# An encoder layer with latent attention in one kernel: x tiles, weight buffers, DMA issuers, output weights and the last norm rearranged

## The chip, the cores and the metric

The kernel runs on one core of a Trainium2 chip. The metric is the device time of one execution in microseconds; a run of the kernel before gives the median of several executions. Beside the times there is a profile of one execution, taken by the hardware profiler.

The engines of a core work side by side, each through its own list of instructions in order: TensorE (PE) for matmuls, VectorE (DVE), ScalarE (ACT), GpSimd (POOL), and SyncE (SP), which here only issues DMAs. ACT can issue DMAs too. PEld in the profile is the load of a matmul's stationary operand. A line L59 is line 59 of the kernel before.

## The reference, cut to what matters

DEPTH is 1, so only the attention layer and the final norm are computed. Input x has 1024 rows of 1024 columns in float32.

```python
h = x + mla_mixer(rms_norm(x, l0_norm), *weights)
return rms_norm(h, final_norm)

def mla_mixer(h, w_in, q_norm, w_uq, kv_norm, w_ukv, w_out):
    proj = h @ w_in                       # c_q 384, c_kv 256, k_pe 64, gate 1024
    q = rms_norm(c_q, q_norm) @ w_uq      # 8 heads of 128 + 64 (rotary)
    kv = rms_norm(c_kv, kv_norm) @ w_ukv  # 8 heads of 128 (key) + 128 (value)
    s = q_nope @ k_nope.T + rope(q_pe) @ rope(k_pe).T
    o = softmax(s * scale) @ v            # not causal
    return (o * silu(gate)) @ w_out
```

rms_norm(y, g) is y * rsqrt(mean(y * y) + 1e-6) * g.

## The kernel before

Every product is made of three matmuls (`mm3`, L58): each float32 operand is split into a high part that the PE's format holds and a low part for the rest, and high x high, high x low and low x high are summed. `split` (L63) does it for a weight: POOL writes the high part, DVE subtracts it for the low one. So each weight goes DMA, POOL, DVE, PE, and has a raw buffer and a pair of split buffers.

The instructions are written down in one order, but a planner puts those of each engine into the order in which they stand in its queue, by a simulated timeline and the written order as priority; a load can go out far ahead of its place in the program once its buffer is free. Buffers are named tiles of pools with a number of copies (`bufs`). Writing a copy again waits until its readers are done.

The stages:

1. **Latent query** (L161 to L186). Eight steps over the 1024 columns of x. Each loads a 128 x 1024 tile of x transposed (`xr`) and 128 x 384 of weights, scales and splits both (ACT writes `xh`, DVE `xl`), and does 18 matmuls into six accumulators. The first tile is loaded and split in two halves, the others whole.
2. **Streams** (`stream`, L251). The other columns of w_in, 128 at a time: two for the latent key and value, one for the rotary key, eight for the gate. Each uses two half weights (`gwh`, `gwl`, in four copies each, pool `gp`), 24 matmuls a half. The latent norms and the rotary queries (`rope_half`, L343, two groups of four heads in two halves of the rows) lie between the gate streams. `load_q(wqp[...])` at L375 loads the rotary weights, two for a group; they share the tags `wq_h`, `wq_l` (two copies) and the raw buffer `w_r` (one copy) with the query and key weights of the heads. `rope_half` stores its results, high and low, to `qpe_d` in DRAM by four DMAs on SP's queue (L362).
3. **Attention** (L634 to L699). 64 units, eight heads of eight row blocks, numbered u. `scores(u)` does 10 matmuls into one of two score buffers, DVE takes the maximum, ACT the exponential (L464), POOL scales, DVE transposes 32 x 32 blocks. After four units `exchange` (L473) finishes the transposition of a group by 16 DMAs on SP's queue, eight for each half `d`. `split_part` (L483) splits `d` on ACT, DVE and POOL, and `values` (L498) multiplies with v. Keys, queries and values of the next head are produced in between. In the second unit of the last head, `load_w_out` (L517) loads and splits all eight half blocks of w_out for the first 512 output columns, on ACT and on DVE or POOL.
4. **Output** (L538 to L630, L700). For each row block and half of the columns: split of the gated heads (`o_split`), 24 matmuls, plus x, sum of squares. The blocks 0 to 3 of the first half start in the last units of attention. The last row block (`out_last`, L606) does its second half in two chunks; behind its last matmul come the sum of squares, the reciprocal root with one Newton step (`rsqrt`, L138), and the scaling and storing of both halves:

```python
v = ss/D + v ; s = sqrt(v) ; r = 1/s             # DVE, ACT, DVE
s = -0.5*r*r ; s = s*v ; r = (s + 1.5)*r         # DVE
```

Of the kernel before, what the change touches and what calls it, by code (L numbers as in the profile page):

```python
# [8 lines left out]
F32 = mybir.dt.float32  # L9
F32R = mybir.dt.float32r  # L10
AF = mybir.ActivationFunctionType
ALU = mybir.AluOpType
AX = mybir.AxisListType

P = 128
# [14 lines left out]
def kernel(  # L30
# [56 lines left out]


    g_sb = const.tile([P, KD + 5], F32, name="g_sb")
    const.tile([P, 72], F32, name="pad_a")  # L90
    qpe_d = dram.tile([H, 4, 32, L], F32, name="qpe_d")

    row_d = {name: dram.tile([P, KD], F32, name=f"{name}_d") for name in ("rx", "sq", "sk", "rq", "rk")}
    kk_h = const.tile([P, L], F32R, name="kk_h")
    kk_l = const.tile([P, L], F32R, name="kk_l")
    ss = const.tile([P, 2, KD], F32, name="ss")
    const.tile([P, 112], F32, name="pad_b")

    def acc(name):
        return ps_a.tile([P, 512], F32, name=name, tag="acc")  # L100
# [15 lines left out]

    xctx = ExitStack()
    xs = xctx.enter_context(tc.tile_pool(name="xs", bufs=1, side="right"))
    gp = xctx.enter_context(tc.tile_pool(name="gp", bufs=4, side="right"))
    xp = xctx.enter_context(tc.tile_pool(name="xp", bufs=1, side="right"))  # L120
    xh = xp.tile([P, KD, L], F32R, name="xh")
    xl = xp.tile([P, KD, L], F32R, name="xl")
# [23 lines left out]
    with ExitStack() as wctx:  # L146
        wp = wctx.enter_context(tc.tile_pool(name="wp", bufs=3))

        idle = wp.tile([P, HT], mybir.dt.bfloat16, name="idle", bufs=1)
        nc.vector.memset(idle, 0.0)  # L150
        warm = ps_t.tile([P, HT], F32, name="warm", tag="t")
        for _ in range(8):
            mm(warm, lhsT=idle[:, 0:P], rhs=idle, start=True, stop=True)
        ones_f = wp.tile([P, P], F32, name="ones_f", bufs=1)
        nc.vector.memset(ones_f, 1.0)
        ones = xs.tile([P, P], F32R, name="ones")
        nc.scalar.copy(ones, ones_f)
        s_a, s_b = wide("s_a"), wide("s_b")
        a_4, a_5 = acc("acc_4"), acc("acc_5")
        accs = [[s_a[:, 0:512], s_a[:, 512:L]], [s_b[:, 0:512], s_b[:, 512:L]], [a_4, a_5]]  # L160
        for k in range(KD):  # L161
            wr = wp.tile([P, QR], F32, name=f"wr_{k}", tag="wr")
            xr = wp.tile([P, L], F32, name=f"xr_{k}", tag="xr")
            if k == 0:
                nc.scalar.dma_start(g_sb, gains)
                nc.sync.dma_start(xr[:, halves(0)], xT[0:P, halves(0)])
                nc.sync.dma_start(wr, wcq[k])
                nc.sync.dma_start(xr[:, halves(1)], xT[0:P, halves(1)])
            else:
                nc.sync.dma_start(wr, wcq[k])  # L170
                nc.sync.dma_start(xr, xT[k * P:(k + 1) * P])
            wh = wp.tile([P, QR], F32R, name=f"wh_{k}", tag="wh")
            wl = wp.tile([P, QR], F32R, name=f"wl_{k}", tag="wl")
            split(wr, wh, wl)
            for hs in [halves(0), halves(1)] if k == 0 else [slice(0, L)]:
                nc.scalar.activation(xh[:, k, hs], xr[:, hs], AF.Copy, scale=g_sb[:, k:k + 1])
                nc.vector.scalar_tensor_tensor(
                    xl[:, k, hs], xr[:, hs], g_sb[:, k:k + 1], f32(xh[:, k, hs]),
                    op0=ALU.mult, op1=ALU.subtract,
                )  # L180
            units = [(m, half) for half in range(2) for m in range(3)]
            if k == KD - 1:
                units = [(m, half) for m in range(3) for half in range(2)]
            for m, half in units:
                ms, hs = slice(m * P, (m + 1) * P), halves(half)
                mm3(accs[m][half], wh[:, ms], wl[:, ms], xh[:, k, hs], xl[:, k, hs], k == 0, k == KD - 1)  # L186

        nc.scalar.copy(craw[0], s_a)
        nc.vector.tensor_copy(craw[1], s_b)
        nc.scalar.copy(craw[2][:, 0:HT], a_4)  # L190
        nc.vector.tensor_copy(craw[2][:, HT:L], a_5)
# [129 lines left out]
    def load_split(shape, src, tag, bufs, pool=None):  # L321
        pool = pool or wts
        wh = pool.tile(shape, F32R, name=f"{tag}_h", tag=f"{tag}_h", bufs=bufs)
        wl = pool.tile(shape, F32R, name=f"{tag}_l", tag=f"{tag}_l", bufs=bufs)
        wr = wts.tile(shape, F32, name=f"{tag}_r", tag="w_r")
        nc.sync.dma_start(wr, src)
        split(wr, wh, wl)
        return wh, wl

    def load_q(src):  # L330
        return load_split([P, 3, P], src, "wq", 2)

    def load_k(h):
        return load_split([P, 2, P], wuk[h], "wk", 1)
# [8 lines left out]
    def rope_half(g, half, w):  # L343
# [8 lines left out]
        for i, (f0, f1, op) in enumerate(((cos, sin, ALU.subtract), (sin, cos, ALU.add))):  # L352
            t, hl = rooms[((g * 2 + half) * 2 + i) % len(rooms)]
            t0, t1 = t[:, 0:HT], t[:, HT:L]
            hi, lo = hl[:, 0:HT], hl[:, HT:L]
            nc.vector.tensor_mul(t0, ab[0], f0)
            nc.vector.tensor_mul(t1, ab[1], f1)
            nc.gpsimd.tensor_tensor(t0, t0, t1, op=op)
            nc.scalar.copy(hi.bitcast(F32R), t0)
            nc.vector.tensor_sub(lo.bitcast(F32R), t0, hi)  # L360
            for c, src in ((i, hi), (2 + i, lo)):
                nc.sync.dma_start(qpe_d[g * 4:(g + 1) * 4, c, :, hs], src)  # L362

    for i in range(1, H):
        stream_gate(i)
# [79 lines left out]
    produce_v(v_now, 0, w_v)  # L445

    square, part = {}, {}

    def scores(u, q, kx, qpe):
        half, qs = (u % 8) // 4, slice((u % 4) * P, (u % 4 + 1) * P)  # L450
# [22 lines left out]
    def exchange(g):  # L473

        src = square.pop(g).rearrange("p j k t c -> p j (k t c)")
        for two in range(2):
            d = part[g, two] = at.tile([P, 2, L], F32, name="d", tag="d")
            for a in range(2):
                for j in range(4):
                    r0 = (two * 2 + a) * 32  # L480
                    nc.sync.dma_start(d[j * 32:(j + 1) * 32, a], src[r0:r0 + 32, j])

    def split_part(g, two):  # L483
        d = part[g, two]
# [113 lines left out]
            nc.vector.scalar_tensor_tensor(v, ss[:, 1, t:t + 1], 1.0 / D, v, op0=ALU.mult, op1=ALU.add)  # L598

    def out_rstd(t):  # L600
        mean_square(t, 1)
        s, r = (columns.tile([P, 1], F32, name=f"y{c}", tag=f"y{c}", bufs=2) for c in "sr")
        rsqrt(ss[:, 0, t:t + 1], s, r)
        return r

    def out_last(t):  # L606
# [17 lines left out]
                mean_square(t, 1)  # L624
        r = out_rstd(t)
        y0 = y_sb[:, t * HT:(t + 1) * HT]
        nc.scalar.mul(y0, y0, r)
        nc.scalar.dma_start(out[ts, halves(0)], y0)
        nc.vector.tensor_scalar(yg, yg, r, 1.0, op0=ALU.mult, op1=ALU.mult)
        nc.sync.dma_start(out[ts, halves(1)], yg)  # L630
    v_of = {0: v_now}
    U = H * 8
    w_q_next, w_k_next = load_q(wqn[1]), load_k(1)
    for u in range(U + 10):  # L634
        h, i = u // 8, u % 8
# [18 lines left out]
        if u % 2 == 0 and u >= 8:  # L654
            g, two = (u - 8) // 4, (u - 8) % 4 // 2
            if g < U // 4:
                values(g, two, v_of[g // 4])
        if u == U + 1:
            y_sb = turned_tile("y_sb").rearrange("p a b -> p (a b)")
            gf_sb = wop.tile([P, D], F32, name="gf_sb")  # L660
            nc.sync.dma_start(gf_sb, gf)
        if u in (U + 1, U + 3):
            started.append(out_start(0, len(started)))
        if u == U + 3:
# [15 lines left out]
            if i in (4, 5, 6):  # L680
                produce_v(v_now, i - 3, w_v)
        if h == H - 1:
            if i == 1:
                for k in range(H):
                    load_w_out(k, 0)
            continue
        if i == 3:
            produce_k(k_next, 0, w_k_next)
# [76 lines left out]
```

## Time and profile before

| | us |
|---|---|
| median of 3 runs | 598.67 (598.4 to 599.02) |
| the profiled execution | 599.3 |
| its span, first to last instruction | 597.3 |
| PE busy in the span | 579.0 |
| DVE, ACT, POOL busy | 433.0, 277.3, 218.9 |
| mean granted clock of PE | 0.992 |

In the timeline a row has the start, the duration, the engine and line, the operation and its tiles, out<-in, with their shape; in brackets stands how long the engine had been idle and what ended that. "x16" says that 16 like instructions are merged into the row. SPq and ACTq are the DMA issues of SP and ACT. A matmul's start is exact, its end is modelled, so matmuls in a row overlap; the time of one is the distance between starts. The list of waits has the engine and line that waited, for whom, the sum in us, how many times, and the longest.

### The profile page before, as it was taken

Reading aid. Unit: us, or ns where it says so; the run is one execution under the profiler, and the core shown is the slowest. Engines: PE = TensorE matmul, PEld = TensorE weight load, DVE = VectorE, ACT = ScalarE, POOL = GpSimd, SP = SyncE. Lnnn points to the kernel's source line nnn. Section 1 sums busy time; section 2 is a strip of 40 time slices with the busy share of each in tenths; the row PEclk is TensorE's granted clock in tenths of the full one; section 3 lists DMA queues with packets and bytes.
Section 4 is the critical chain, followed back from the end, with each engine's and each line's share of the span. In section 5 each row is a group of like instructions: output and inputs, shape, how many; then the busy total and the mean of one; then the engine's idle time right before and its main releaser. Section 6 shows DMA issues by size and latency. Waiting matters only on the chain.

```text
span 597.3 us, 8664 instructions
## 1 busy us (share of the span) xinstructions
PE 579.0 (97%) x2988; PEld 494.0 (83%) x2988; DVE 433.0 (72%) x632; ACT 277.3 (46%) x435; POOL 218.9 (37%) x195
## 2 busy tenths in 40 slices
PE   8999999979999998999999999999999989999995
PEld 5888888858888887888988989888888968978885
DVE  5813579926205889899878899898987996783663
ACT  4347553111103464456454545454545673653642
POOL 3414504514101344544334354434442662563000
PEclk9999999979999999999999999999999999999999
DMA  8846322233202166466654747456646975431332
GB/s 300 277 128 233 106 75 68 64 143 109 108 18 71 40 160 146 110 148 153 145 128 107 180 107 160 93 115 166 143 93 138 275 174 141 120 104 53 124 140 105
DMA packets 35534, 78.71 MB, mean 132 GB/s; under 512 B 7266, under 2 KB 10850, under 8 KB 35428
## 3 DMA queue, kind: packets, MB, share of 16 engines
q1 hardware_dynamic: 34196, 76.08, 47.3%
q10 hardware_dynamic: 1296, 2.10, 1.0%
q8 instruction: 23, 0.38, 0.3%
q14 instruction: 19, 0.16, 0.1%
HBM read 36.19 MB, written 8.41 MB: 75 GB/s over the span
## 4 chain that ended last, share of the span: by engine, by line
PE 77%; DVE 8%; DMA 6%; issue 3%; SPq 2%; ACT 2%; POOL 0%; ACTq 0%; DVEq 0%; POOLq 0%
PE s L59 4%; PE s L60 4%; PE s L456 4%; PE pv L59 4%; PE s L457 4%; PE s L61 4%; PE pv L60 4%; PE pv L61 4%; PE o L61 4%; PE o L60 4%; PE g L59 4%; PE g L60 4%; PE o L59 4%; PE g L61 4%; PE q L60 2%
## 5 line engine op out<-in xcount | busy, mean ns | idle before, releaser
L470 POOL TENSOR_SCALAR probs<-probs,rc 128x1024 f32<-128x1024 f32 x64 | 80.9, 1268 | 111.0 <-DVE rc L469 85.3
L464 ACT ACTIVATE probs<-s,nmx 128x1024 f32<-128x1024 f32 x64 | 71.3, 1114 | 72.8 <-DVE nmx L462 69.5
L489 ACT CAST pt_h<-d 128x1024 fp32r<-128x1024 f32 x64 | 66.0, 1051 | 46.3 <-PE pv L61 19.9
L471 DVE STREAM_TRANSPOSE probs<-probs 128x1024 f32<-128x1024 f32 x64 | 78.9, 1233 | 6.5 <-POOL probs L470 5.9
L462 DVE TENSOR_REDUCE nmx<-s 128x1 f32<-128x1024 f32 x64 | 76.9, 1207 | 7.5 <-PE s L457 7.4
L59 PE MATMUL pv<-pt_h,v_h 128*128 128x256 f32 x256 | 72.6, 284 | 2.3 <-ACT pt_h L489 2.3
L60 PE MATMUL pv<-pt_l,v_h 128*128 128x256 f32 x256 | 72.5, 283 | 0.6 <-DVE pt_l L491 0.5
L61 PE MATMUL pv<-pt_h,v_l 128*128 128x256 f32 x256 | 72.4, 283 | 0.0
L494 POOL TENSOR_TENSOR pt_l<-d,pt_h 128x512 fp32r<-128x512 f32 x32 | 46.0, 1438 | 46.1 <-ACT pt_h L489 29.4
L59 PE MATMUL g<-xh,gwh 128*128 128x512 f32 x160 | 62.8, 392 | 0.0
L60 PE MATMUL g<-xl,gwh 128*128 128x512 f32 x160 | 62.7, 392 | 0.0
L61 PE MATMUL g<-xh,gwl 128*128 128x512 f32 x160 | 62.5, 391 | 0.0
L59 PEld LDWEIGHTS pv<-pt_h,v_h 128*128 128x128 f32 x256 | 48.9, 191 | 4.4 <-ACT pt_h L489 3.2
L59 PE MATMUL s<-k_h,q_h 128*128 128x512 f32 x128 | 50.1, 394 | 1.9 <-ACT probs L464 1.9
L60 PEld LDWEIGHTS pv<-pt_l,v_h 128*128 128x128 f32 x256 | 48.9, 191 | 2.9 <-DVE pt_l L491 0.8
L61 PEld LDWEIGHTS pv<-pt_h,v_l 128*128 128x128 f32 x256 | 48.9, 191 | 2.0
L60 PE MATMUL s<-k_l,q_h 128*128 128x512 f32 x128 | 50.3, 393 | 0.0
L456 PE MATMUL s<-kk_h,qpe 128*128 128x512 f32 x128 | 50.2, 392 | 0.0
L457 PE MATMUL s<-kk_l,qpe 128*128 128x512 f32 x128 | 50.1, 391 | 0.0
L61 PE MATMUL s<-k_h,q_l 128*128 128x512 f32 x128 | 49.9, 390 | 0.0
L491 DVE TENSOR_TENSOR pt_l<-d,pt_h 128x1024 fp32r<-128x1024 f32 x32 | 45.1, 1410 | 5.2 <-ACT pt_h L489 4.6
L60 PE MATMUL o<-wol,o_split 128*128 128x512 f32 (+1 forms) x118 | 44.8, 379 | 0.0
(191 smaller groups left out, 1293.0 us busy)
## 6 DMA issues: line engine op xcount, KB each, us to landing
d<-probs SPq DMA_DIRECT2D x256, 128.0 KB
gwr<-in_wg SPq DMA_DIRECT2D x20, 256.0 KB
craw_b<-in_x SPq DMA_DIRECT2D x8, 512.0 KB
qpe<-qpe_d SPq DMA_DIRECT2D x16, 256.0 KB
wor<-in_wo SPq DMA_DIRECT2D x16, 256.0 KB
xr<-in_x SPq DMA_DIRECT2D x16, 256.0 KB
xr<-in_xT SPq DMA_DIRECT2D x7, 512.0 KB
qpe_d<-craw_a SPq DMA_DIRECT2D x8, 256.0 KB
```

The costliest lines, as they stand in the source:

```text
L59: mm(ps, lhsT=lh, rhs=rh, start=first, stop=False)
L60: mm(ps, lhsT=lh, rhs=rl, start=False, stop=False)
L61: mm(ps, lhsT=ll, rhs=rh, start=False, stop=last)
L456: mm(s[:, ks], lhsT=qpe_s, rhs=kk_h[:, ks], start=False, stop=False)
L457: mm(s[:, ks], lhsT=qpe_s, rhs=kk_l[:, ks], start=False, stop=True)
L462: nc.vector.tensor_reduce(nmx, s, axis=AX.X, op=ALU.max, negate=True)
L464: nc.scalar.activation(p_t.rearrange("p j k c -> p k j c"), s.rearrange("p (k j c) -> p k j c", k=8, j=4), AF.Exp, bias=nmx, accum_out=sm,)
L470: nc.gpsimd.tensor_scalar(p_t, p_t, rc, 1.0, op0=ALU.mult, op1=ALU.mult)
L471: nc.vector.transpose(out=p_t, in_=p_t)
L489: nc.scalar.copy(hi, src)
L491: nc.vector.tensor_sub(lo, src, f32(hi))
L494: nc.gpsimd.tensor_sub(lo[:, 1], src[:, 1], f32(hi[:, 1]))
```

## The change

- The second and third x tile are loaded and split in halves, as the first was.
- The raw buffer `w_r` has two copies instead of one, the split buffers `wq_h` and `wq_l` four instead of two. The gate weights `gwh`, `gwl` have three copies instead of four. Two pads are replaced by one that is smaller.
- ACT issues the stores of the rotary queries, and half of the exchange of the first and of the last group (eight of 16 DMAs each).
- The output weights of the first half are loaded one for each unit from the second unit of the last head on, the last one at the first step behind attention.
- The reciprocal root of the output norm: ACT takes the root with the sum of squares and the part already there as scale and bias, and DVE adds them up for itself. The Newton step is `(v*r*r - 3)*r`, which is -2 times the former result; `gf_sb` is multiplied by -0.5 once on POOL to make up for it.
- For the last row block, DVE scales the second half first; of the first half, ACT scales and stores 320 columns, and POOL scales 192, which SP stores.

```diff
-    const.tile([P, 72], F32, name="pad_a")
+    ss = const.tile([P, 2, KD], F32, name="ss")
+    const.tile([P, 56], F32, name="pad")
...
-    ss = const.tile([P, 2, KD], F32, name="ss")
-    const.tile([P, 112], F32, name="pad_b")
...
-    gp = xctx.enter_context(tc.tile_pool(name="gp", bufs=4, side="right"))
+    gp = xctx.enter_context(tc.tile_pool(name="gp", bufs=3, side="right"))
...
-                nc.sync.dma_start(xr, xT[k * P:(k + 1) * P])
+                for hs in [halves(0), halves(1)] if k < 3 else [slice(0, L)]:
+                    nc.sync.dma_start(xr[:, hs], xT[k * P:(k + 1) * P, hs])
...
-            for hs in [halves(0), halves(1)] if k == 0 else [slice(0, L)]:
+            for hs in [halves(0), halves(1)] if k < 3 else [slice(0, L)]:
...
-        wr = wts.tile(shape, F32, name=f"{tag}_r", tag="w_r")
+        wr = wts.tile(shape, F32, name=f"{tag}_r", tag="w_r", bufs=2)
...
-        return load_split([P, 3, P], src, "wq", 2)
+        return load_split([P, 3, P], src, "wq", 4)
...
-                nc.sync.dma_start(qpe_d[g * 4:(g + 1) * 4, c, :, hs], src)
+                nc.scalar.dma_start(qpe_d[g * 4:(g + 1) * 4, c, :, hs], src)
...
-                    nc.sync.dma_start(d[j * 32:(j + 1) * 32, a], src[r0:r0 + 32, j])
+                    queue = nc.scalar if a and g in (0, U // 4 - 1) else nc.sync
+                    queue.dma_start(d[j * 32:(j + 1) * 32, a], src[r0:r0 + 32, j])
...
     def out_rstd(t):
+        s, r = (columns.tile([P, 1], F32, name=f"y{c}", tag=f"y{c}", bufs=2) for c in "sr")
+        v = ss[:, 0, t:t + 1]
+        nc.scalar.activation(s, ss[:, 1, t:t + 1], AF.Sqrt, bias=v, scale=1.0 / D)
         mean_square(t, 1)
-        s, r = (columns.tile([P, 1], F32, name=f"y{c}", tag=f"y{c}", bufs=2) for c in "sr")
-        rsqrt(ss[:, 0, t:t + 1], s, r)
+        nc.vector.reciprocal(r, s)
+        nc.vector.scalar_tensor_tensor(s, r, v, r, op0=ALU.mult, op1=ALU.mult)
+        nc.vector.scalar_tensor_tensor(r, s, -3.0, r, op0=ALU.add, op1=ALU.mult)
         return r
...
         y0 = y_sb[:, t * HT:(t + 1) * HT]
-        nc.scalar.mul(y0, y0, r)
-        nc.scalar.dma_start(out[ts, halves(0)], y0)
         nc.vector.tensor_scalar(yg, yg, r, 1.0, op0=ALU.mult, op1=ALU.mult)
         nc.sync.dma_start(out[ts, halves(1)], yg)
+        first, second = slice(0, 320), slice(320, HT)
+        nc.scalar.mul(y0[:, first], y0[:, first], r)
+        nc.scalar.dma_start(out[ts, first], y0[:, first])
+        nc.gpsimd.tensor_scalar(y0[:, second], y0[:, second], r, 1.0, op0=ALU.mult, op1=ALU.mult)
+        nc.sync.dma_start(out[ts, second], y0[:, second])
...
+        if u == U:
+            load_w_out(H - 1, 0)
         if u == U + 1:
...
             nc.sync.dma_start(gf_sb, gf)
+            nc.gpsimd.tensor_scalar(gf_sb, gf_sb, -0.5, 1.0, op0=ALU.mult, op1=ALU.mult)
...
         if h == H - 1:
-            if i == 1:
-                for k in range(H):
-                    load_w_out(k, 0)
+            if i:
+                load_w_out(i - 1, 0)
             continue
```

More of the change, by code (lines that the diff above doesn't have):

```diff
@@ L447 @@
     square, part = {}, {}
+    U = H * 8
     def scores(u, q, kx, qpe):
@@ L626, in out_last @@
         y0 = y_sb[:, t * HT:(t + 1) * HT]
-        nc.scalar.mul(y0, y0, r)
-        nc.scalar.dma_start(out[ts, halves(0)], y0)
         nc.vector.tensor_scalar(yg, yg, r, 1.0, op0=ALU.mult, op1=ALU.mult)
         nc.sync.dma_start(out[ts, halves(1)], yg)
+        first, second = slice(0, 320), slice(320, HT)
[3 more added lines that the diff above has]
+        nc.sync.dma_start(out[ts, second], y0[:, second])
     v_of = {0: v_now}
-    U = H * 8
     w_q_next, w_k_next = load_q(wqn[1]), load_k(1)
```

## The prediction, on record before the result

> **What bounds the kernel now.** I read the page first, then who waited for whom on TensorE, then the busy time by stage, and last the timeline of each place in which TensorE stands still.
>
> ```profile
> span 597.3 us, 8664 instructions
> PE 579.0 (97%) x2988; PEld 494.0 (83%) x2988; DVE 433.0 (72%) x632; ACT 277.3 (46%) x435; POOL 218.9 (37%) x195
> ```
>
> TensorE (PE) is busy for 579.0 of 597.3 us, so 18.3 us of standing still is all that a change which leaves the matmuls alone can take, besides matmuls that run slowly. The waits of PE name what ended each stop:
>
> ```profile
> PE ab L59 <- POOL wq_h L64: 4.4, 1, 4.4
> PE pv L59 <- ACT pt_h L489: 2.3, 2, 1.2
> PE s L59 <- ACT probs L464: 1.9, 2, 1.2
> PE warm L153 <- DVE idle L150: 1.2, 1, 1.2
> PE s_a L59 <- ACT xh L176: 0.7, 1, 0.7
> PE pv L60 <- DVE pt_l L491: 0.5, 1, 0.5
> PE s_a L60 <- DVE xl L177: 0.5, 1, 0.5
> ```
>
> These are 11.5 us; the rest is mostly the tail after the last matmul. By stage (columns: length, then busy PE, PEld, DVE, ACT, POOL, the granted clock, DMA share, GB/s):
>
> ```profile
> 120.00:140.00 20.00, 15.63 (x57) 12.37 (x56) 6.80 (x10) 1.68 (x2) 2.65 (x4) 0.83 0.36 128
> 220.00:240.00 20.00, 18.10 (x98) 15.32 (x98) 18.68 (x28) 10.33 (x16) 9.51 (x8) 1.00 0.54 123
> 460.00:480.00 20.00, 20.00 (x123) 17.79 (x121) 17.68 (x25) 13.44 (x21) 11.38 (x9) 1.00 0.89 251
> 480.00:500.00 20.00, 17.10 (x96) 14.64 (x96) 18.86 (x26) 12.47 (x19) 12.36 (x9) 1.00 0.64 159
> ```
>
> The 4.4 us lie in 120:140, 1.9 us in 220:240, 2.9 us in 480:500. Only in the first is the granted clock below 1.00. So the four places that the change touches are the start, the rotary weights, the two ends of attention, and the tail.
>
> **The rotary weights (more buffers).** This is the largest term.
>
> ```profile
> 123.10 0.39 PE L60 MATMUL g<-xl,gwh 128*128 128x512 f32 x1
> 123.33 0.39 PE L61 MATMUL g<-xh,gwl 128*128 128x512 f32 x1
> 128.08 0.79 PE L59 MATMUL ab<-cq_h,wq_h 128*128 128x512 f32 x1 [4.37 <-POOL wq_h L64]
> ...
> 134.16 0.39 PE L61 MATMUL g<-xh,gwl 128*128 128x512 f32 x1
> ```
>
> Two matmuls in a row start 0.23 us apart. From 128.08 to 134.16 lie 14 steps in 6.08 us, 0.43 us each: about half speed. Had PE run on, the 15th matmul after 123.33 would have started at 123.33 + 15 x 0.23 = 126.8; it starts at 134.16. The stop costs 7.4 us: 4.4 of waiting and some 3.0 of slow matmuls behind it. The Trainium skill (TensorE: Matmul & The Clock Gate, "What's actually happening") says that an idle window of about 3.4 us halves the clock; the trace agrees, since the 4.37 us stop is followed by half speed and the stops of 1.2 us are not.
>
> The first of the four rotary loads on SP's queue, the last one in the chain that ended last, and a stage of the stop:
>
> ```profile
> 8.79 0.44 SPq L326 DMA_DIRECT2D wq_r<-in_wqp  x1
> ```
> ```profile
> 116.33 11.04 DMA wq_r<-in_wqp
> ```
> ```profile
> 124.00:126.00 2.00, 0.00 (x0) 0.00 (x0) 0.00 (x0) 0.62 (x1) 0.00 (x0) 1.00 0.26 103
> ```
>
> The last load goes out at 116.33 only because the single raw buffer and the two split buffers were taken, and it lands 11.04 us later, behind the qpe_d stores on the same queue: in 124:126 the DMA engines are busy at a share of 0.26, with 103 GB/s, as though 4 of 16 worked. The first such load goes out at 8.79, far ahead of its place in the program, so the planner hoists loads as soon as a buffer is free. With four split pairs and two raw buffers no load has to wait for a matmul of the first group; all four can be loaded and split long before 120. The stores go to ACT, so they hold back no load on SP. There they are 16 issues, at most 10 us by the 0.63 us each that the exchange shows below, and those of the low parts wait for DVE; behind them stand casts of the next half and Silu, whose results no matmul takes before attention. ACT does 1.68 of 20 us in 120:140, which covers it; without that cover it would be up to 10 us. What is late next in 120:140? DVE has 6.80 of 20 us to do, ACT 1.68, and the products' buffers are free by then; I find nothing, and take -7.4 us. Bounds: 0 (a new wait there as long) and -7.5.
>
> **The gate weights in three buffers instead of four** are the price of that room.
>
> ```profile
> 96.83 0.64 POOL L64 TENSOR_SCALAR gwh<-gwr 128x512 fp32r<-128x512 f32 x1 [4.37 <-PE g L60]
> 103.44 1.53 DVE L65 TENSOR_TENSOR gwl<-gwr,gwh 128x512 fp32r<-128x512 f32 x1
> ```
>
> POOL splits as soon as PE releases a buffer. Half a gate stream is 24 matmuls, 24 x 0.23 = 5.5 us. With four buffers a released one is needed again three halves later (16.6 us), with three two halves later (11.0 us). The slowest pair above takes from 96.83 to 103.44 + 1.53 = 104.97, 8.1 us. That leaves 2.9 us, so I take 0. Bounds: 0 and +1.5 (POOL comes 4.4 us late, the time that it is idle here, and 2.9 of it is spare). It cannot gain, since nothing starts sooner with fewer buffers.
>
> **Start: the second and third x tile in halves.**
>
> ```profile
> 5.54 0.72 ACT L176 ACTIVATE xh<-xr,g_sb 128x512 fp32r<-128x512 f32 x1 [1.14 <-DMA xr<-in_xT]
> ...
> 8.53 1.15 ACT L176 ACTIVATE xh<-xr,g_sb 128x1024 fp32r<-128x1024 f32 x1 [2.27 <-DMA xr<-in_xT]
> ```
>
> PE waits 0.7 us for the second tile's xh and 0.5 us for its xl, 1.2 in all. A half takes ACT 0.72 instead of 1.15 us, so even if no byte comes earlier its first half is ready 0.43 us sooner, and its bytes are half as many. The two added issues on SP cost up to 0.44 us each (the row at 8.79) and push the next loads by 0.9 us; the waits list nothing for the tiles after the third. I take -1.0, between -1.2 and +0.4 (the second tile's other half behind one more issue).
>
> **Exchanges of the first and the last group, half of each issued by ACT.** exchange moves one group's probabilities by 16 DMAs. The first group's at 207, the last group's at 501, what stands on ACT and PE near them, and a stage of the last one:
>
> ```profile
> 207.02 10.13 SPq L481 DMA_DIRECT2D d<-probs  x16
> ...
> 208.76 1.11 ACT L464 ACTIVATE probs<-s,nmx 128x1024 f32<-128x1024 f32 x1 [4.26 <-DVE nmx L462]
> ...
> 211.02 0.39 PE L59 MATMUL s<-k_h,q_h 128*128 128x512 f32 x1
> ...
> 501.06 10.04 SPq L481 DMA_DIRECT2D d<-probs  x16
> ...
> 501.86 0.62 ACT L566 CAST o_split<-gate 128x512 fp32r<-128x512 f32 x1 [3.03 <-PE o L60]
> ```
> ```profile
> 503.00:505.00 2.00, 2.00 (x10) 1.67 (x9) 0.20 (x1) 0.00 (x0) 0.00 (x0) 1.00 0.94 207
> ```
>
> 16 issues take 10.04 us, 0.63 each, which looks as if SP were the limit and two queues would halve it. But while they go out the DMA engines are busy at a share of 0.94: the data are the limit, and issuing waits for them. So I expect the exchange to take about 10 us still. Were issuing the limit, the exchange would take 5 us and at best the 1.9 us of stops in 220:240 would go. The Trainium skill (DMA: Bandwidth & Descriptors, "Issuing engines are not separate DMA queues") speaks against that reading: all issuers feed the same engines, and a second one saves only the issuer's time. The share of 0.94 sides with it; by this rule the two moves bring nothing to the sum, by the issue row alone up to -1.9 us.
>
> What it adds: 8 issues on ACT are 8 x 0.63 = 5.0 us in which everything behind them waits. In the first group that is the Exp at 208.76. If all eight go first, from 207.0, Exp starts at 212.0, 3.3 us late; it ends at 208.76 + 1.11 = 209.9 now and frees the score bank that PE takes at 211.02, 1.1 us later, so PE would stand up to 2.2 us. If the planner puts Exp first, nothing. I take +0.5, between -1.9 and +2.2. The lower end is that -1.9. In the last group the cast at 501.86 stands behind; 501.06 + 5.0 = 506.1 makes it 4.2 us late: 0 to +4.2. PE is busy for 2.00 of 2.00 us in 503:505 with other products, and this cast's is one of several, so I stay near the lower end: +0.5.
>
> **Output weights spread over the last head.** Before, eight loads and splits come at once, and the stage 460:480 shows the DMA engines at 0.89.
>
> ```profile
> 478.22 1.05 ACT L489 CAST pt_h<-d 128x1024 fp32r<-128x1024 f32 x1 [2.72 <-DMA d<-probs]
> ...
> 481.16 1.14 ACT L534 CAST woh<-wor 128x512 fp32r<-128x512 f32 x2
> 482.21 1.10 ACT L464 ACTIVATE probs<-s,nmx 128x1024 f32<-128x1024 f32 x1
> ```
>
> ACT waits 2.72 us for late probabilities, then casts output weights, and Exp comes at 482.21 behind them; PE's stops of 0.5 (pt_l) and 1.2 us (probs) follow from it. With one weight per unit both can go: -1.7. The third stop in 480:500, 1.2 us on pt_h, hangs on an exchange and on DVE, which is busy for 18.86 of 20 us and has no less to do; I keep it. Bounds: -2.9 (all of it) and +1 (a weight cast just ahead of a late Exp).
>
> **Tail.**
>
> ```profile
> 591.77 0.16 DVE L598 SCALAR_TENSOR_TENSOR ss<-ss 128x1 f32<-128x1 f32 x1
> ...
> 592.79 0.16 DVE L144 SCALAR_TENSOR_TENSOR yr<-ys,yr 128x1 f32<-128x1 f32 x1
> 593.04 0.72 ACT L627 ACTIVATE y_sb<-y_sb,yr 128x512 f32<-128x512 f32 x1 [0.87 <-DVE yr L144]
> 593.80 0.34 ACTq L628 DMA_DIRECT2D out_y<-y_sb  x1
> ```
>
> From 591.77 to 592.79 six small steps follow each other, 0.20 us apart; the change makes it five (the square root takes the mean square in itself, one multiply goes): -0.2. The scaling of 512 columns (0.72 us) becomes 320 on ACT, about 0.5, and 192 on POOL beside it; the third output DMA comes behind another issue on SP (0.34), so of the 0.2 gained about half is left. I take -0.3, between -0.6 and 0. The added scaling of gf_sb on POOL falls near 503:505, where POOL does 0.00 of 2.00: 0.
>
> **The sum:** -7.4 - 1.0 + 0.5 + 0.5 - 1.7 - 0.3 = -9.4 us. The profiled execution took 599.3 us (597.3 of span); it would take 589.9. The median of the runs is 598.67, so the forecast is 589.3 us. About 0.2%, 1.2 us, can be told from no change.
>
> **Rivals.**
> (1) Another wait takes the stop's place at 123: the next weight or store is late by 3 to 4 us instead of 4.4, or the ACT-issued moves cost their upper bounds (2.2 + 4.2). For it: DVE splits a gate weight 6 us after POOL (the rows at 96.83 and 103.44), and the planner puts issues of equal readiness in the program's order, exchange first. Against: DVE does 6.80 of 20 us in 120:140. With a stop of 3.5 us and the clock kept: 589.3 + 3.5 = 592.8; with both upper bounds in place of 0.5 + 0.5: 589.3 + 5.4 = 594.7; together at most 597.
> (2) Everything goes: all stops of attention too. 589.3 - 1.0 (no cost of ACT's issues) - 1.9 (220:240) - 1.2 (the third stop in 480:500) = 585.2, and 584.7 with start and tail at their best. For it: stops in attention come from late data. Against: DVE at 18.7 and 18.9 of 20 us there.
> (3) Slower: the three gate buffers. If POOL's and DVE's split of a half takes more than 11.0 us, each half stream waits; PE goes at the pace of POOL and DVE. At 11.8 us, 0.8 us for each of the 16 halves of eight gates, it is 12.8 us: 602.1. It decides from 11.7 us on (16 x 0.66 = 10.6 eats the gain and 1.2 more); the rows show 8.1.
> (4) The planner doesn't hoist the loads, and the stop stays: -2 at most, 597 to 598.7. The load at 8.79 speaks against it.
>
> **How the numbers follow.** The forecast with its own bounds, 587 to 592.5: 0.62. (2): 0.14. (1): 0.16. (3): 0.05. (4): 0.03. Faster is the forecast, (2), and most of (1): 0.91; same is (4) with the edge of (1): 0.04; slower is (3): 0.05. The range 585 to 595 leaves out the ends of (1) and (2), and (3) and (4).
>
> **What would show it.** Right: no wait of PE on wq_h, granted clock 1.00 in 120:140; start waits under 0.3 us; an exchange that still lands about 10 us after it began; PE idle for some 1.2 us in all of 480:500 instead of 2.9; five steps between the last square sum and the last scaling. Wrong: a PE wait on gwh or gwl (rival 3), a stop of over 2 us on probs or o_split behind ACT's issues (rival 1), or an exchange that takes 5 us.

## The result and the profile after

The changed kernel takes 613.07 us in the median of 4 runs (612.36 to 613.48); the kernel before took 598.85 us beside it (598.40 to 599.05). The ratio is 1.0237, with an interval of 1.0220 to 1.0255. The forecast was 589.3 us; the change makes the kernel 14.2 us slower.

The head of the page of the kernel after, and its list of PE's waits (engine and line that waited, for whom: sum in us, how many times, the longest):

```profile
span 611.6 us, 8643 instructions
PE 582.7 (95%) x2988; PEld 495.4 (81%) x2988; DVE 434.6 (71%) x626; ACT 277.3 (45%) x437; POOL 224.8 (37%) x197
```
```profile
PE s L59 <- ACT probs L465: 10.6, 3, 7.9
PE ab L59 <- DVE craw_a L356: 3.8, 1, 3.8
PE pv L59 <- ACT pt_h L491: 2.8, 3, 2.0
PE warm L152 <- DVE idle L149: 1.2, 1, 1.2
PE o L59 <- ACT o_split L568: 1.2, 1, 1.2
PE s_a L59 <- POOL wh L64: 0.2, 1, 0.2
```

The number of matmuls is the same, but PE is busy 3.7 us longer and stands still for 28.9 us instead of 18.3: 10.6 + 3.7 = 14.3 us, the difference of the spans. Three waits that the prediction named are gone: on `wq_h` (4.4), on `xh` (0.7) and on `xl` (0.5). No wait on a gate weight has come. In their place a single stop of 7.9 us stands on ACT's Exp, and one of 3.8 us where the 4.4 had been. The stages that hold these stops, in the kernel after (length, busy PE, PEld, DVE, ACT, POOL, the granted clock, DMA share, GB/s):

```profile
0.00:20.00 20.00, 18.61 (x74) 13.22 (x75) 12.43 (x17) 8.79 (x11) 7.68 (x14) 1.00 0.89 301
120.00:140.00 20.00, 16.55 (x66) 13.52 (x67) 13.62 (x19) 3.98 (x5) 8.90 (x9) 0.91 0.31 99
200.00:220.00 20.00, 12.06 (x52) 9.76 (x52) 9.84 (x14) 7.42 (x11) 5.10 (x6) 0.83 0.57 131
240.00:260.00 20.00, 17.95 (x91) 15.14 (x90) 16.20 (x22) 9.16 (x14) 7.55 (x8) 0.91 0.62 140
480.00:500.00 20.00, 16.89 (x100) 14.35 (x98) 17.25 (x22) 10.74 (x18) 11.88 (x8) 1.00 0.79 198
500.00:520.00 20.00, 18.54 (x96) 15.65 (x96) 14.74 (x22) 7.97 (x13) 8.38 (x5) 1.00 0.63 153
```

The stage length less PE's busy time is how long PE stood. Summed over the places of the change:

| PE stands still, us | before | after | difference |
|---|---|---|---|
| start (0 to 20) | 2.45 | 1.39 | -1.1 |
| rotary weights (100 to 140) | 4.37 | 3.80 | -0.6 |
| first exchange and behind it (200 to 260) | 1.90 | 10.28 | +8.4 |
| end of attention (480 to 560) | 3.02 | 6.95 | +3.9 |
| behind the last matmul | 6.56 | 6.47 | -0.1 |

The longer busy time is in part the clock. Before, one stretch of matmuls ran at half speed, the 14 steps of 0.43 instead of 0.23 us behind 128.08, some 3.0 us lost. After, there are three, each with some 3.4 us of matmuls at half speed, 1.7 us lost: from 123.8 to 127.2, from 215.95 to 219.4 and from 243.3 to 246.7. That is 5.1 us, 2.1 more than before; the rest of the 3.7 us was not traced. Two of the three lie behind the first exchange. (The granted clock of a stage counts half speed during a stop as well: it is 0.64 in 212:214 already, where PE stands, so the 0.83 of 200:220 is more than the matmuls lost.)

The largest stop, in the timeline of the kernel after (start, duration, engine and line, operation; in brackets how long the engine was idle before, and what ended that):

```profile
206.11 1.18 DVE L463 TENSOR_REDUCE nmx<-s 128x1 f32<-128x1024 f32 x1
206.26 7.59 SPq L483 DMA_DIRECT2D d<-probs  x8
...
206.27 8.32 ACTq L483 DMA_DIRECT2D d<-probs  x8
...
214.69 1.11 ACT L465 ACTIVATE probs<-s,nmx 128x1024 f32<-128x1024 f32 x1 [11.29 <-DMA d<-probs]
...
215.95 0.79 PE L59 MATMUL s<-k_h,q_h 128*128 128x512 f32 x1 [7.94 <-ACT probs L465]
```

The maximum that Exp needs is there at 206.11 + 1.18 = 207.29. Exp starts at 214.69, when the last of ACT's eight issues is out; they take 8.32 us, 1.04 each, not the 0.63 of one queue. PE wanted the score buffer at 215.95 - 7.94 = 208.0 and gets it when Exp ends. The profile puts Exp's wait down to these DMAs. In the last group the planner put casts between, four issues and four:

```profile
512.50 10.06 SPq L483 DMA_DIRECT2D d<-probs  x8
512.51 3.79 ACTq L483 DMA_DIRECT2D d<-probs  x4
...
516.63 1.05 ACT L491 CAST pt_h<-d 128x1024 fp32r<-128x1024 f32 x1 [6.55 <-issue]
...
520.08 3.19 ACTq L483 DMA_DIRECT2D d<-probs  x4
```

The stop near 123 is of another kind. The chain of waits of the kernel after, from 97 to 130, has the two small transfers that turn the row of the latent key's norm (`rk_d`):

```profile
101.40 5.66 DMA rk_d<-small
...
107.08 6.33 DMA gate<-rk_d
...
113.43 1.30 DVE craw_a L249
```

DVE waits 10.25 us for the second of them, and the rotary product that PE wants at 119.7 comes at 123.45. In the kernel before, the same two were issued at 89.46 and 91.57, and the first rotary store at 111.58. Now the first rotary store is issued at 100.00, ahead of the first row transfer at 101.40. The row transfers are also some 12 us later than before, and they are so with the buffers alone (102.49 in experiment 9).

### The profile page after: what moved, and what is told of

It reads as the page before. It is cut to its first block, busy times and chain, and to the rows that moved or that the text cites. A ratio compares the mean times of both kernels' runs of the same rounds, so it can differ in the third digit from the quotient of the medians.

```text
span 611.6 us, 8643 instructions
## 1 busy us (share of the span) xinstructions
PE 582.7 (95%) x2988; PEld 495.4 (81%) x2988; DVE 434.6 (71%) x626; ACT 277.3 (45%) x437; POOL 224.8 (37%) x197
## 4 chain that ended last, share of the span: by engine, by line
PE 70%; DVE 8%; DMA 7%; issue 5%; POOL 4%; ACT 2%; ACTq 1%; SPq 1%; POOLq 0%; DVEq 0%
PE s L60 4%; PE s L457 4%; PE s L59 4%; PE s L458 4%; PE s L61 4%; PE pv L59 4%; PE g L60 4%; PE g L61 4%; PE g L59 4%; PE pv L61 4%; PE pv L60 4%; PE o L61 3%; PE o L59 3%; PE o L60 3%; DMA d<-probs 2%
## 5 line engine op out<-in xcount | busy, mean ns | idle before, releaser
L496 POOL TENSOR_TENSOR pt_l<-d,pt_h 128x512 fp32r<-128x512 f32 x32 | 48.9, 1528 | 44.2 <-ACT pt_h L491 37.8
L59 PE MATMUL s<-k_h,q_h 128*128 128x512 f32 x128 | 50.9, 399 | 10.6 <-ACT probs L465 10.6
L493 DVE TENSOR_TENSOR pt_l<-d,pt_h 128x1024 fp32r<-128x1024 f32 x32 | 43.5, 1358 | 9.9 <-ACT pt_h L491 8.4
L59 PE MATMUL o<-woh,o_split 128*128 128x512 f32 (+1 forms) x118 | 44.9, 382 | 2.1 <-ACT o_split L568 1.2
## 6 DMA issues: line engine op xcount, KB each, us to landing
craw_b<-in_x SPq DMA_DIRECT2D x8, 512.0 KB
xr<-in_xT SPq DMA_DIRECT2D x5, 512.0 KB
```

The costliest lines, as they stand in the source:

```text
L59: mm(ps, lhsT=lh, rhs=rh, start=first, stop=False)
L493: nc.vector.tensor_sub(lo, src, f32(hi))
L496: nc.gpsimd.tensor_sub(lo[:, 1], src[:, 1], f32(hi[:, 1]))
```

## The experiments

Three theories stood against each other. **ACT**: the issues on ACT hold it for as long as their data take, and what stands behind them in its queue, Exp and casts, comes late. **SPREAD**: the output weights in every unit of the last head cost time instead of saving it. **The prediction's**: the terms of its sum are right, and the loss is due to another thing, a plan that fits worse with more buffers among them. Experiments 1, 3, 4 and 5 take the change apart one part at a time; 2, 6, 9, 10 and 12 add one part to the kernel before; 7, 8 and 11 change how a part is made.

**1. The first exchange back on SP.**

```diff
-                    queue = nc.scalar if a and g in (0, U // 4 - 1) else nc.sync
+                    queue = nc.scalar if a and g in (U // 4 - 1,) else nc.sync
```

> The changed kernel with only one part undone: the first group's exchange goes out on SP alone again. Theory ACT (in the changed kernel the eight issues hold ACT for 8.32 us, from 206.27 to 214.6, and Exp, which frees the score buffer, stands behind them; PE stops for 7.94 us and then runs slowly for some 3 us more): the stop goes, 613.1 - 10.5 = 602.5 us, and no wait of PE on probs over 1 us near 210. Theory ORDER (the planner's new order of matmuls, given by the buffers, leaves PE without other work there, and ACT is only where it shows): the stop moves to another releaser and the time stays above 609.

Measured: 599.97 us (10 runs), beside 599.17 of the kernel before, ratio 1.0018 (1.0000 to 1.0036). Against the 613.07 of the whole change, 13.1 us are gone with eight issues. In its list of PE's waits the 7.9 us are no more, and the stop near 123 stays:

```profile
PE ab L59 <- DVE craw_a L356: 3.7, 1, 3.7
PE pv L59 <- ACT pt_h L491: 2.1, 3, 1.1
PE s L59 <- ACT probs L465: 1.4, 2, 0.7
```

PE stands 8.6 us less between 200 and 260, and the clock is 1.00 in both stages that showed 0.83 and 0.91, so the two stretches at half speed, 1.7 us each, are gone too: 12.0 of the 13.1.

**2. The first exchange on ACT, alone on the kernel before.**

```diff
-                    nc.sync.dma_start(d[j * 32:(j + 1) * 32, a], src[r0:r0 + 32, j])
+                    queue = nc.scalar if a and g in (0,) else nc.sync
+                    queue.dma_start(d[j * 32:(j + 1) * 32, a], src[r0:r0 + 32, j])
```

> The kernel before with one part alone: ACT issues eight of the first exchange's 16 DMAs. Theory ACT: a new stop of PE on probs near 208 of 6 to 8 us with slow matmuls behind it, against 1.9 us of stops there now: 598.8 + 7 to 10 = 606 to 609. Theory ORDER: 598 to 600, since the order that leaves PE empty comes from the buffers. By my prediction (2.2 us at the most): 600.5.

Measured: 606.88 us, ratio 1.0135 (1.0111 to 1.0160). The same picture stands in ACT's timeline:

```profile
206.97 8.53 ACTq L484 DMA_DIRECT2D d<-probs  x8
215.54 1.11 ACT L466 ACTIVATE probs<-s,nmx 128x1024 f32<-128x1024 f32 x1 [11.10 <-DMA d<-probs]
...
216.80 0.80 PE L59 MATMUL s<-k_h,q_h 128*128 128x512 f32 x1 [5.68 <-ACT probs L466]
```

So the loss belongs to this part and doesn't need the others. PE stops at 216.80 - 5.68 = 211.12, when it took the buffer before (211.02): Exp is 215.54 - 208.76 = 6.8 us late, 1.1 us of it is covered, and 5.7 us remain. The loss is 7.7 us here and 13.1 in the changed kernel: here the longest stop is 5.7 us instead of 7.9, and the changed kernel has a second one of 2.05 us at 243 with slow matmuls behind it, which this kernel has not. There ACT's cast of `pt_h` waits until 242.21 for the second group's exchange, which SP began to issue at 235.28; why the plan leaves PE no other work then was not settled.

**3. Both exchanges back on SP.**

```diff
-                    queue = nc.scalar if a and g in (0, U // 4 - 1) else nc.sync
-                    queue.dma_start(d[j * 32:(j + 1) * 32, a], src[r0:r0 + 32, j])
+                    nc.sync.dma_start(d[j * 32:(j + 1) * 32, a], src[r0:r0 + 32, j])
```

> The changed kernel with both exchanges on SP alone; ACT still issues the rotary stores. If ACT's issues in the last exchange (four in 3.8 us at 512.5, four in 3.2 us at 520.1, with casts of pt_h and o_split behind them) cause the stops between 500 and 535, it is 2 to 3 us faster than the run with only the first undone. If the spread of the output weights causes them, it is as fast within 1 us, and PE's stops between 480 and 560 stay near 7 us.

Measured: 597.67 us, ratio 0.9980 (0.9968 to 0.9991): 2.3 us less than experiment 1.

**4. The rotary stores back on SP as well**, so that ACT issues what it issued before.

```diff
-                nc.scalar.dma_start(qpe_d[g * 4:(g + 1) * 4, c, :, hs], src)
+                nc.sync.dma_start(qpe_d[g * 4:(g + 1) * 4, c, :, hs], src)
```

> The changed kernel with no DMA moved to ACT: both exchanges and the rotary stores on SP. If the stop on the products (ab, 3.8 us at 119.6, granted clock 0.91 behind it) comes from the stores that ACT issues ahead of the small row transfers of the latent key's norm (5.66 and 6.33 us long there), it goes and this is 5 to 6 us faster than the run with both exchanges undone. If it comes from the buffers (the first rotary group is taken up earlier, and its stores stand before the row transfers whoever issues them), the stop stays within 2 us of 3.8 and the two runs are alike.

Measured: 593.57 us, ratio 0.9915 (0.9899 to 0.9932): 4.1 us less than experiment 3. The order of SP's queue shows why (timeline of SP):

```profile
101.37 0.33 SPq L209 DMA_DIRECT2D rk_d<-small  x1
101.79 0.61 SPq L362 DMA_DIRECT2D qpe_d<-craw_a  x1
102.78 0.33 SPq L210 DMA_DIRECT2D gate<-rk_d  x1
103.16 0.54 SPq L362 DMA_DIRECT2D qpe_d<-craw_a  x1
```

On one queue the first row transfer goes ahead of the stores, and its second step is issued 1.41 us behind it, instead of 5.38 in experiment 3. PE's stop near 123 shrinks from 3.3 to 0.9 us, and the clock in 120:140 goes from 0.91 to 1.00.

**5. The spread output weights undone too.** What is left of the change: start, buffers, tail.

```diff
-        if u == U:
-            load_w_out(H - 1, 0)
...
-            if i:
-                load_w_out(i - 1, 0)
+            if i == 1:
+                for k in range(H):
+                    load_w_out(k, 0)
```

> The changed kernel with no DMA moved to ACT and with the output weights loaded at once again; left are the x halves, the buffers and the tail. The run with no issue on ACT took 593.57 us, and its PE stood for 1.8 + 1.9 + 0.1 + 0.6 = 4.4 us in 460:540, against 2.9 + 0.1 = 3.0 in the kernel before. If the spread costs (theory SPREAD: a weight split per unit stands ahead of Exp and pt_h in every unit), this is about 1.4 us faster, 592.2. By my prediction, where the spread takes 1.7 us away, it is slower, 595.3.

Measured: 592.21 us, ratio 0.9887 (0.9865 to 0.9908). The interval touches that of experiment 4, so in this chain the 1.4 us of the spread are a direction only. The waits on `o_split` (1.5 and 0.4 us in experiment 4) are gone; those on `pt_h` grow from 1.4 to 3.9 us. No kernel here is clearly faster: it is 7.1 us below the one before in the medians (599.28 beside it), and experiments 9 and 11 are equal to it within the noise.

**6. The spread alone on the kernel before** (the edit of 5 in the other direction).

> The kernel before with one part alone: the output weights spread over the last head. By my prediction 1.7 us faster than before, 597.2. By theory SPREAD 1.4 us slower, 600.3.

Measured: 600.44 us, ratio 1.0022 (1.0007 to 1.0038), 12 runs. It saves nothing. Its stage at the end of attention:

```profile
480.00:500.00 20.00, 16.16 (x90) 13.86 (x91) 20.00 (x26) 12.80 (x20) 13.13 (x9) 1.00 0.64 159
```

DVE is now busy for 20.00 of 20.00 us where it had 18.86, PE stands 3.8 instead of 2.9 us there, and 1.2 us in 500:520 where it stood for none. But the edit spread the weights in the written order only, hardly in the plan. The loads near 474, in the kernel before:

```profile
473.92 8.12 SPq L519 DMA_DIRECT2D wor<-in_wo  x5
```

And in this one, with two rows of ACT (lines shifted by two):

```profile
473.92 8.36 SPq L521 DMA_DIRECT2D wor<-in_wo  x5
...
481.41 0.62 ACT L536 CAST woh<-wor 128x512 fp32r<-128x512 f32 x1
481.93 1.10 ACT L466 ACTIVATE probs<-s,nmx 128x1024 f32<-128x1024 f32 x1
```

Four loads go out near 462 in both, five at 473.92, three from 492 on. Of the four casts ahead of Exp one has moved behind it.

**7. The first exchange on ACT, but its issues later in the plan**, so that Exps stand between them.

```diff
+                    tc.cur_priority += 150 * (queue is nc.scalar)
                     queue.dma_start(d[j * 32:(j + 1) * 32, a], src[r0:r0 + 32, j])
+                    tc.cur_priority -= 150 * (queue is nc.scalar)
```

> The kernel before with the first exchange's eight issues on ACT as in the run with that part alone (606.88), but with a later place in the planner's order: ACT does them in parts of at most three, with Exp between them. If the cost is that Exp waits behind eight issues in a row, PE's stop of 5.7 us there shrinks to at most 3 (three issues of about 1 us), with full clock behind it: 599 to 602. If issues on ACT cost as such (8 us of its time, or slower transfers), it stays at 605 or more.

Measured: 599.03 us beside 599.28, ratio 1.0000 (0.9985 to 1.0015). ACT's timeline (two lines of code more, so the lines are shifted):

```profile
205.79 1.51 ACTq L485 DMA_DIRECT2D d<-probs  x2
207.40 1.12 ACT L466 ACTIVATE probs<-s,nmx 128x1024 f32<-128x1024 f32 x1 [4.22 <-DVE nmx L464]
...
209.66 1.12 ACT L466 ACTIVATE probs<-s,nmx 128x1024 f32<-128x1024 f32 x1 [0.56 <-DVE nmx L464]
209.66 1.67 ACTq L485 DMA_DIRECT2D d<-probs  x2
```

The same eight issues from the same engine cost nothing that can be told when they stand among the Exps in ones and twos instead of all ahead of one. The loss is the order, not the issuing; and moving half an exchange to ACT gains nothing either.

**8. The rotary stores on ACT in another layout** (experiment 3 with `qpe_d` arranged so that a store is one block of 128 rows; each load becomes four).

```diff
-    qpe_d = dram.tile([H, 4, 32, L], F32, name="qpe_d")
+    qpe_d = dram.tile([4, H, 32, L], F32, name="qpe_d")
...
-                nc.scalar.dma_start(qpe_d[g * 4:(g + 1) * 4, c, :, hs], src)
+                nc.scalar.dma_start(qpe_d[c, g * 4:(g + 1) * 4, :, hs].rearrange("h p t -> (h p) t"), src)
...
-            nc.sync.dma_start(f32(qpe), qpe_d[h, :, :, halves(half)].rearrange("c p t -> (c p) t"))
+            for c in range(4):
+                nc.sync.dma_start(f32(qpe[c * 32:(c + 1) * 32]), qpe_d[c, h, :, halves(half)])
```

> As the run with both exchanges on SP (597.67), ACT still issuing the rotary stores, but qpe_d lies with the part (high or low, first or second half) as its slowest dimension, so that a store is one block of 128 rows instead of four blocks of 32; the loads become four DMAs each. If the small row transfers are late because each store keeps few DMA engines busy for long (103 GB/s at a share of 0.26 in the kernel before), the row transfers take 1.5 and 4 us again, the stop on ab goes below 1 us and the time to 593 to 594. If they are late only because ACT's stores come first, the stop stays near 3.3 us and the time near 597.7.

Measured: 594.61 us, ratio 0.9923 (0.9901 to 0.9946), 3.1 us less than experiment 3 with the stores still on ACT. The stop near 123 is gone; its stage there, and one late in attention with a new stop:

```profile
120.00:140.00 20.00, 20.00 (x90) 16.57 (x89) 14.77 (x20) 4.62 (x6) 9.12 (x9) 1.00 0.54 175
460.00:480.00 20.00, 16.41 (x93) 14.68 (x92) 14.97 (x20) 10.80 (x17) 12.22 (x8) 0.85 0.72 193
```

The second row transfer is issued 1.42 us behind the first (103.43 and 102.01), and DVE waits 5.2 us for it instead of 9.8 in experiment 3. So what the stores on ACT cost is that they go ahead of the small transfers and, in the old layout, are slow.

**9. The buffers alone on the kernel before.**

```diff
-    gp = xctx.enter_context(tc.tile_pool(name="gp", bufs=4, side="right"))
+    gp = xctx.enter_context(tc.tile_pool(name="gp", bufs=3, side="right"))
...
-        wr = wts.tile(shape, F32, name=f"{tag}_r", tag="w_r")
+        wr = wts.tile(shape, F32, name=f"{tag}_r", tag="w_r", bufs=2)
...
-        return load_split([P, 3, P], src, "wq", 2)
+        return load_split([P, 3, P], src, "wq", 4)
```

> The kernel before with one part alone: the weight buffers (two raw, four split pairs, three gate pairs, one pad). My prediction's term for it is -7.4 us at the rotary weights and 0 at the gate weights: 591.5. If the earlier first rotary group costs, as in the run with no issue on ACT (a stop of 0.9 us on ab), it is -6.5: 592.5. If three gate pairs stop PE (rival 3), a wait of PE on gwh or gwl shows and it is above 595.

Measured: 592.44 us beside 599.03, ratio 0.9890 (0.9868 to 0.9912), 6.6 us in the medians. Two of its stages:

```profile
120.00:140.00 20.00, 19.37 (x86) 15.69 (x84) 12.59 (x18) 4.29 (x6) 7.49 (x7) 1.00 0.34 111
460.00:480.00 20.00, 18.23 (x102) 15.95 (x101) 16.30 (x23) 13.48 (x23) 14.41 (x10) 0.91 0.84 237
```

In 120:140 PE stands 0.63 us instead of 4.37, at full clock; no wait on a gate weight is listed.

**10. The last exchange alone on the kernel before** (the edit of 2 with the last group).

> The kernel before with one part alone: ACT issues half of the last exchange. By my prediction +0.5 (0 to +4.2), 599.3. By the two runs with and without it in the changed kernel (599.97 and 597.67) +2.3, 601.1, with new stops of PE on pt_h or o_split between 500 and 535.

Measured: 603.06 us, ratio 1.0073 (1.0044 to 1.0101), 4.0 us in the medians. ACT's timeline:

```profile
500.96 8.46 ACTq L484 DMA_DIRECT2D d<-probs  x8
509.62 1.99 ACT L492 CAST pt_h<-d 128x1024 fp32r<-128x1024 f32 x2 [10.75 <-DMA d<-probs]
511.52 1.73 ACT L569 CAST o_split<-gate 128x512 fp32r<-128x512 f32 x5
```

Alone, the planner puts all eight ahead; the split of the gated heads, which started at 501.86, starts at 511.52, 9.7 us later, and PE stands 2.15 us in 500:520 and 0.97 in 520:540 where it stood 0 and 0.1.

**11. Experiment 5 with the layout of 8, stores on SP.**

> The fastest so far (592.21: x halves, buffers and tail; no issue on ACT, output weights at once) with the rotary stores laid out as one block of 128 rows. The stop of 0.8 us on ab goes: 591.4. If the loads in four pieces each crowd the exchanges, it is 592 to 594.

Measured: 592.44 us, ratio 0.9889 (0.9871 to 0.9908), no different from experiment 5. PE's last 0.8 us of waiting on the rotary halves are gone, and waits of 2.2 us on Exp, where there were 0.6, take their place late in attention.

**12. Start and tail alone on the kernel before.**

> The kernel before with the first x tiles in halves and the shorter chain of the last norm, nothing else of the change. By the prediction the start gives 1.0 us and the tail 0.3: 1.3 us below the kernel before, about 597.5. The rival is what the best version so far suggests (592.2, where the buffers alone gave 592.4): the stage 0 to 20 us loses its 1.0 us of idle all the same, but work that is shifted by it meets a wait later on and the whole gives 0 to 0.4 us.

Measured: 597.93 us beside 598.88, ratio 0.9981 (0.9968 to 0.9995), 0.95 us in the medians. That is nearer to the prediction's 1.3 than to the rival's 0 to 0.4, but the interval reaches from 0.3 to 1.9 us and doesn't exclude the rival; PE stands 1.19 us in 0:20 instead of 2.45.

## Why the prediction was wrong, point by point

| part | forecast, us | alone on the kernel before | taken out of the changed kernel |
|---|---|---|---|
| buffers (with the gate's three) | -7.4 | -6.6 (exp. 9) | not by itself |
| start and tail | -1.3 | -0.95 (exp. 12) | not by itself |
| first exchange on ACT | +0.5 | +7.7 (exp. 2) | +13.1 (exp. 1) |
| last exchange on ACT | +0.5 | +4.0 (exp. 10) | +2.3 (exp. 3) |
| rotary stores on ACT | 0 | not tried | +4.1 (exp. 4) |
| output weights spread (in the written order) | -1.7 | +1.2 (exp. 6) | +1.4, not resolved (exp. 5) |

**The step that failed is "8 issues on ACT are 8 x 0.63 = 5.0 us in which everything behind them waits", with its "between -1.9 and +2.2".** The sentence before it had said that the data are the limit and that issuing waits for them. By that reading an engine that issues half of the same data is held until nearly all of it has gone, whatever its number of issues; the 0.63 us were the pace of one queue that had the data to itself. Two queues share them, an issue takes 1.04 us, and ACT is held for 8.3 to 8.5 us. In experiment 2 this size alone makes the stop 5.7 us instead of 2.2; the slack of 1.1 us held there. In the changed kernel the slack failed too: it was taken from the plan of before, in which Exp waited for its maximum until 208.76. In the changed kernel the maximum is there at 207.29, PE wants the buffer at 208.0, and nothing of the 8.3 us is covered. A stop so long also brings slow matmuls, which the upper bound left out: 1.7 us behind it in the changed kernel, 2.3 in experiment 2 (half speed from 216.8 to 221.3). The prediction did name the planner's order ("all eight first") as the bad case; it weighted it too low, and its upper bound of 2.2 us was less than a third of the 7.7 us that the part costs alone.

**The last exchange**: the mechanism was right, the price and the choice near the lower end were not. That the 4.0 us of experiment 10 (interval 2.6 to 6.1) lie at the bound of +4.2 is luck: the bound was a cast 4.2 us late behind 5.0 us of issues, and it came 9.7 us late behind 8.5 us of them and two casts of `pt_h`; PE stood 3.0 us more for it. "PE is busy for 2.00 of 2.00 us in 503:505" said nothing of 506 to 512, when the split stands behind the issues.

**The rotary stores on ACT**: cover was sought for what stands behind them on ACT, and ACT has that cover. What was not asked is what the stores run ahead of. With more buffers the planner takes the first rotary group up some 12 us earlier (its first store goes out at 100.00 instead of 111.58), and on a queue of their own its stores start before the row transfers of the latent key. The chain from there, row transfer, DVE, rotary half, PE, gives back 3.8 us of the stop that the buffers had taken away. The row "0.26, 103 GB/s", which the prediction had read as 4 of 16 engines at work, was the hint; experiment 8 shows it by taking the stop away with another layout. By the Trainium skill (DMA: Bandwidth & Descriptors, Why a DMA increments its semaphore by 16 and not by 1) the slowest dimension of an access decides how many engines share a transfer; the outer 4 of these stores and the 128 rows of experiment 8 behave that way here (a DMA share of 0.26 and 89 GB/s in 104:105 of experiment 3, 0.57 and 207 GB/s in 103:104 of experiment 8).

**The spread**: the waits of 480:500 were put down to ACT's casts of output weights ahead of Exp. The step that failed is "with one weight per unit both can go": there is no one weight per unit. The planner hoists a load as soon as a buffer is free, as the prediction says of the rotary weights, and the raw tile `wor` has four copies, so the loads go out in fours and fives as before (in the changed kernel in fours, at 472.88, 485.06 and 503.37). In experiment 6 the stop on Exp shrinks from 1.2 to 0.7 us, the one on `pt_h` grows from 1.2 to 2.3. The cast that ends the latter stands behind an Exp that starts at 489.51 instead of 487.70, since DVE takes its maximum at 488.29 instead of 486.40: the low part of an output weight ahead of it takes 1.45 us instead of 0.68, and a transposition (487.14) is now ahead of it too. DVE had 18.86 of 20 us to do there before and has 20.00 now. That DVE's order is the cause is read from these rows; no run changed DVE's work alone, and what weights that really come one by one would do, no run shows.

**What was right**: the buffers, with the size (-7.4 forecast, -6.6 measured; part of the difference can lie in 460:480, where PE stands 1.8 us and the clock is 0.91); no wait on the gate weights, so rival 3 is out; no wait on `wq_h`, so rival 4 is; 1.1 us of idle time less at the start. The tail is 0.1 us shorter (from the last product's addition to the end 6.54 us before, 6.43 after) instead of 0.3. The addition of the terms itself was not the fault: without the parts on ACT and the spread, whose forecast is 598.67 - 7.4 - 1.3 = 590.0, the kernel takes 592.2.

Of the rivals, (1) had the mechanism, "ACT-issued moves cost their upper bounds" and another wait at 123, and ended at 597 because its prices were the 0.63 us ones; its sign, "a stop of over 2 us on probs", came true. A slower kernel had a chance of 0.05, and that was given to the gate weights, which cost nothing that shows. Of the signs of being right, the granted clock of 1.00 in 120:140 (0.91) and PE idle for 1.2 us in 480:500 (3.1) did not come. "An exchange that still lands about 10 us after it began" did, as far as the runs show (some 11 us from the first issue to the last data, before and in experiment 10; see the last section). So the reading of the DMA share of 0.94 was right, and the step that followed it didn't keep to it.

## What to carry to other kernels

An engine that issues transfers whose data are the limit was held here for most of the transfer (8.3 to 8.5 us), not for its share of the issues at the pace of one queue (5.0). Ask what in-order compute stands behind the issues; with one or two ahead of each instruction that another engine waits for, the loss was gone. When more buffers let work start earlier, look at what its transfers now run ahead of. A change of the written order is not yet a change of the plan: find the moved loads in the trace before crediting them.

## What the runs showed of the hardware

**A second queue got the issues out sooner, not the data.** One queue took 10.04 and 10.13 us for the issues of 16 x 128 KB in the kernel before, at a DMA share of 0.94. With half of them issued from ACT in a row, all were out after 8.32, 8.53 and 8.46 us (the kernel after and experiments 2 and 10). The data took as long. The end of the last exchange, first in the kernel before, then in experiment 10:

```profile
507.00:512.00 5.00, 5.00 (x39) 4.77 (x38) 2.83 (x5) 2.14 (x3) 1.07 (x1) 1.00 0.94 209
512.00:513.00 1.00, 0.98 (x8) 0.77 (x8) 0.72 (x3) 0.65 (x3) 0.68 (x1) 1.00 0.31 62
```
```profile
507.00:512.00 5.00, 4.29 (x31) 3.86 (x29) 0.78 (x3) 2.38 (x3) 0.26 (x1) 1.00 0.98 222
512.00:513.00 1.00, 0.03 (x1) 0.03 (x1) 1.00 (x2) 1.00 (x5) 1.00 (x1) 1.00 0.01 0
```

In the five us ahead of that both move 198 GB/s. So the 2.1 MB that start at 502 are through by some 512.3 with one queue and by 512.0 with two. The Trainium skill (DMA: Bandwidth & Descriptors, "Issuing engines are not separate DMA queues") says that a second issuer saves only sequencer time, usually small beside the transfer; the first half fits this trace, but the issue time isn't small here: 8.3 to 8.5 us on ACT, beside some 10 us of data.

**ACT's issues run beside the ACT instruction ahead of them, and block those behind.** In experiment 7 an issue and an Exp start together at 209.66, one of 1.67 us and one of 1.12.

**How long a stop must be before the clock falls is not one number.** A stop of 3.7 us left the clock at 1.00 (experiment 1, 120:140), and so did one of 2.7 us (experiment 5, 480:500). One of 4.37 us was followed by some 3.0 us of loss (before), and one of 2.05 us by a clock of 0.57 and 1.7 us of loss. The same stop on `wq_h`, 4.1 to 4.7 us long, left the stage at 0.83 in two profiles (before, experiment 12) and at 0.91 in four (experiments 2, 6, 7, 10). The stages behind the stop of 2.05 us, in the kernel after:

```profile
243.00:245.00 2.00, 1.70 (x5) 1.41 (x6) 1.72 (x2) 2.00 (x3) 0.72 (x1) 0.57 0.92 207
245.00:247.00 2.00, 2.00 (x7) 1.56 (x6) 1.44 (x3) 1.40 (x4) 1.28 (x2) 0.58 0.86 175
247.00:249.00 2.00, 2.00 (x10) 1.62 (x9) 1.01 (x2) 1.54 (x2) 1.59 (x2) 1.00 0.31 118
```

The Trainium skill (TensorE: Matmul & The Clock Gate, "What's actually happening") gives an idle window of about 3.4 us, free-running, as the condition; 3.7 us without a loss fits a window that need not line up with the stop, but 2.05 us with a loss doesn't fit a whole idle window. So in these runs a stop of 2 to 5 us cost from nothing to some 3 us more.
